# Reading the moving operands of all large products from the last column to the first

## The chip, the cores and the metric

The kernel runs on one core of a Trainium2 chip. A core has a matrix engine (TensorE, PE in the profile, with its weight loads shown apart as PEld), a vector engine (DVE), a scalar engine (ACT), GpSimd (POOL) and SyncE (SP), which issues transfers. They share a scratch memory of 128 partitions (SBUF); TensorE writes its results into an accumulation memory (PSUM) of eight banks of 512 fp32 per partition. The metric is the time of one execution on the device in microseconds (us), the median of several runs.

## The reference

A decoder trunk of two layers for one sequence of 256 tokens with 2048 features, in fp32. Layer 0 mixes tokens with a gated DeltaNet, layer 1 with HGRN2; each mixer and each SwiGLU feed-forward network (FFN, inner width 5632) stands behind an RMS norm and adds to the residual.

```python
def gdn_mixer(h, w_in, conv_w, a_log, dt_bias, head_norm, w_out):
    proj = h @ w_in                      # 2048 -> 12352: q, k, v, z, b, a
    qkv = silu(causal_depthwise_conv(proj[..., :GDN_CONV_DIM], conv_w))
...
    o = gated_delta_rule_chunked(q, k, v, beta, g)
    o = rmsnorm(o, head_norm) * silu(z)
    return o.reshape(B, S, GDN_VAL_DIM) @ w_out

def hgrn2_mixer(h, w_in, lower_bound, head_norm, w_out):
    proj = h @ w_in                      # 2048 -> 8192: q, f, i, gate
...
    return o.reshape(B, S, HGRN_VAL_DIM) @ w_out

def swiglu(h, w_gate, w_up, w_down):
    return (silu(h @ w_gate) * (h @ w_up)) @ w_down
```

Nearly all arithmetic is in these products with weight matrices; the recurrences between them are small products.

## The kernel before

Every weight is streamed once from HBM in tiles of 128 partitions by 1024 columns (`raw`, 512 KB). ACT rounds a tile to TensorE's fast fp32 form (`wh`, type fp32r), and DVE takes the difference, `wl = raw - wh`, in the same form. Activations are split alike into a high and a low half: `xt_h`, `xt_l` for the normed input, `hth`, `htl` for the FFN's inner activations, `ot_h`, `ot_l` for a mixer's output. A product of precise fp32 is then three fast matmuls that accumulate: high by high, high by low, low by high.

In a matmul one operand, the stationary one (128 columns), is loaded into TensorE, and the other, the moving one, is streamed past it column by column; each of its columns gives one column of the output. Each matmul of this kernel brings its own load. There are two forms of large products:

- Rows (`mm_rows`, line 624; `mm_apart`, line 639, calls it in another order for the last group): the stationary operand is 128 tokens of the activations, the moving one 512 columns of the weights. The output has tokens on partitions and features along the row. FFN, the v and z parts of the gated DeltaNet, the v and gate parts of HGRN2, and both output projections are made so. One tile of 1024 columns is two blocks of 512 features with 128 inputs each, so it feeds 2 blocks x 2 halves of the tokens x 3 = 12 matmuls.
- Columns (`mm_cols`, line 652): the stationary operand is 128 features of the weights, the moving one all 256 tokens of the activations. The output has features on partitions and tokens along the row. The q and k parts of the gated DeltaNet and the q and f parts of HGRN2 are made so, with 24 matmuls to a tile.

A third form, `mm_gates`, makes 48 matmuls for the gates. The other products (`aux` tiles) are small and mostly in plain fp32.

The function `layout` (on the host, before the launch) arranges the weights so that each tile is one contiguous block: `tiles` for input projections and FFN, `out_rows` for output projections.

The program is recorded first and then ordered: `Recorder` notes every operation with the region of the tile that it reads or writes (`Virtual.region`, line 107), derives who depends on whom, and plans the order on each engine from estimated costs. The large products keep the order in which they were written; the rest is fitted around them. All operations are issued at one place, line 490, so in the profile nearly every instruction has that line, and groups are told apart by the names of their tiles.

Weight tiles lie in padded buffers (`PAD`, 64 elements), and `make` chooses the offset within the padding: one for tiles of rows products, and one for each half in columns products (`IN_COLS = {"wh": 224, "wl": 512}`, bytes).

These are the three lines of the large products' operands, rows first:

```python
out = ps[tt] if isinstance(ps, tuple) else ps[:, tt, :]
out, s[:, tok], w[:, cols],
ps[:, f // 2, (f % 2) * T : (f % 2 + 1) * T], w[:, at : at + P], s,
```

The second argument is the stationary operand, the third the moving one.

Of the kernel before, what the change touches and what calls it, by code (L numbers as in the profile page):

```python
# [17 lines left out]
P = 128  # L18
T = 256
D = 2048  # L20
# [70 lines left out]
class Virtual:  # L91
# [15 lines left out]
    def region(self, ap):  # L107
        p0, f0 = divmod(ap.offset, self.row)
        p1, f1 = p0 + 1, f0 + 1
        for step, n in ap.ap:  # L110
            if step % self.row:
                f1 += (n - 1) * step
            else:
                p1 += (n - 1) * (step // self.row)
        if f1 > self.row:
            p1, f0, f1 = p1 + (f1 - 1) // self.row, 0, self.row
        if self.pool.space == PSUM:
            return 0, P, 0, self.row
        return p0, p1, f0, f1
# [387 lines left out]
class Trunk:  # L507
# [116 lines left out]
    def mm_rows(self, ps, i, wh, wl, n_chunks, operand, halves=range(2)):  # L624

        for k in range(2):
            xh, xl = operand(2 * i + k)
            cols = slice(k * 512, (k + 1) * 512)
            for tt in halves:
                tok = slice(tt * P, (tt + 1) * P)  # L630
                out = ps[tt] if isinstance(ps, tuple) else ps[:, tt, :]
                for m, (s, w) in enumerate(((xh, wh), (xh, wl), (xl, wh))):
                    self.nc.tensor.matmul(
                        out, s[:, tok], w[:, cols],
                        start=(i == 0 and k == 0 and m == 0),
                        stop=(i == 2 * n_chunks - 1 and k == 1 and m == 2),
                    )
# [14 lines left out]
    def mm_cols(self, ps, i, wh, wl, n_k, n_f, n_chunks):  # L652

        for k in range(n_k):
            kt = i * n_k + k
            xh, xl = self.operand(kt)
            for f in range(n_f):
                at = (k * n_f + f) * P
                for m, (w, s) in enumerate(((wh, xh), (wh, xl), (wl, xh))):
                    self.nc.tensor.matmul(  # L660
                        ps[:, f // 2, (f % 2) * T : (f % 2 + 1) * T], w[:, at : at + P], s,
                        start=(kt == 0 and m == 0 and f % 2 == 0),
                        stop=(i == 2 * n_chunks - 1 and k == n_k - 1 and m == 2),
                        skip_group_check=True,
                    )
# [10 lines left out]
    def operand(self, kt):  # L676
        return self.xt_h[kt // 4][:, kt % 4, :], self.xt_l[kt // 4][:, kt % 4, :]
# [1004 lines left out]
def layout(inputs):  # L1682
    f = lambda n: np.ascontiguousarray(inputs[n])
    out = {}
    x = f("x").reshape(T, D)
    out["x"] = np.ascontiguousarray(x.reshape(2, P, 4, 512).transpose(2, 1, 0, 3))
    cols = lambda v: v.reshape(16, P).T
    ffn_norm = f("ffn_norm")
    norms = [cols(v) for v in (f("gdn_norm")[0], ffn_norm[0], f("hgrn_norm")[0], ffn_norm[1])]
    out["head"] = np.concatenate([np.eye(P, dtype=np.float32)] + norms, 1)  # L1690

    def tiles(w):
        k, g, _ = w.shape
        return np.ascontiguousarray(
            w.reshape(k // 512, 4, P, g, 512).transpose(3, 0, 2, 1, 4)
        ).reshape(g, k // 512, P, 2048)

    for j in range(2):
        gate, up = f("ffn_w_gate")[j], f("ffn_w_up")[j]
        out[f"ffn_gu{j}"] = tiles(  # L1700
            np.stack([gate.reshape(D, N_FF, T), up.reshape(D, N_FF, T)], 2).reshape(D, N_FF, 512)
        )
        lo = 0
        for part, n in enumerate(FF_PARTS):
            rows = f("ffn_w_down")[j][lo * T : (lo + n) * T]
            out[f"ffn_d{j}_{part}"] = tiles(rows.reshape(n * T, 4, 512))
            lo += n
    w = f("gdn_w_in")[0]
    heads = lambda lo: w[:, lo : lo + D].reshape(D, 8, 2, P)
    out["gdn_kq"] = tiles(np.stack([heads(D), heads(0)], 3).reshape(D, 8, 512))  # L1710
    out["gdn_v"] = tiles(w[:, 2 * D : 4 * D].reshape(D, 8, 512))
    out["gdn_z"] = tiles(w[:, 4 * D : 6 * D].reshape(D, 8, 512))
    ba = w[:, 6 * D :].reshape(16, P, 64)
    out["gdn_ba"] = np.ascontiguousarray(ba.transpose(1, 0, 2)).reshape(P, 1024)

    def out_rows(w):
        k = w.shape[0] // 1024
        return np.ascontiguousarray(
            w.reshape(k, 2, 4, P, 4, 512).transpose(0, 4, 1, 3, 2, 5)
        ).reshape(k, 4, 2, P, 2048)  # L1720

    out["gdn_out"] = out_rows(f("gdn_w_out")[0])
    conv = f("gdn_conv")[0]
    out["gdn_conv"] = np.ascontiguousarray(conv[:, : 2 * D].reshape(4, 32, P).transpose(2, 1, 0))
    out["gdn_conv_v"] = np.ascontiguousarray(conv[:, 2 * D :])
    gate = np.stack([f("gdn_a_log")[0], f("gdn_dt_bias")[0]], 1)
    out["gdn_gate"] = np.concatenate([np.zeros_like(gate), gate], 0)
    out["gdn_hn"] = f("gdn_head_norm").reshape(P, 1)
    p, k = np.arange(P)[:, None, None], np.arange(8)[None, :, None]
    out["unit"] = (4 * k + p // 32 == np.arange(32)[None, None, :]).astype(np.float32)  # L1730
    j, i = np.arange(P)[:, None], np.arange(P)[None, :]
    out["hgrn_in"] = tiles(f("hgrn_w_in")[0].reshape(D, 16, 512))
    out["hgrn_out"] = out_rows(f("hgrn_w_out")[0])
    out["hgrn_hn"] = f("hgrn_head_norm").reshape(P, 1)
    out["hgrn_lb"] = np.ascontiguousarray(f("hgrn_lower_bounds").reshape(2, 16, P).transpose(2, 0, 1))
    c = np.arange(CH)[None, :]
    out["masks"] = np.stack(
        [((j >= c // s * 2 * s) & (j < c // s * 2 * s + s)).astype(np.float32) for s in MASKED], 1
    )
    out["final_norm"] = f("final_norm").reshape(1, D)  # L1740
    return out
# [19 lines left out]
```

## Time and profile before

| what | value |
|---|---|
| median of 3 runs | 2774.8 us (2774.77 to 2776.47) |
| span of the profiled execution, first to last instruction | 2773.0 us |
| its mean granted TensorE clock | 0.999 |
| DMA, mean over the span | 209 GB/s, 580.52 MB |

The profile is one execution. Its span leaves out what lies before the first and after the last instruction, 1.8 us against the median. The busy table gives for each engine its busy time, the share of the span and the number of instructions. The chain is the work that ended last, followed back from the end: the engine with the largest share of it sets the time. Groups of instructions show "busy us, mean ns of one | idle time before them, and what ended it". Matmuls are pipelined: one may start while the one before it is still under way, so a group's mean duration is more than what one matmul adds to the time, and the distance from start to start (the pitch) is what counts. Pieces of the chain in order of time are given as start, length, what, and how many instructions.

### The profile page before, as it was taken

How to read it: one execution, taken by the hardware profiler on the slowest of the kernel's cores; microseconds unless marked ns; L12 is line 12 of the kernel's file. 1: busy time of each engine (PE TensorE's matmuls, PEld its weight loads, DVE VectorE, ACT ScalarE, POOL GpSimd, SP SyncE). 2: the span in 40 equal slices, each digit the busy share in tenths (PEclk: the TensorE clock that was granted, in tenths of full speed). 3: DMA queues.
4: the chain of work that ended last, by engine and by line, in shares of the span. 5: the costliest groups of instructions: out<-in, count | busy, mean ns of one | idle time of the engine just before them, and what ended most of it. 6: DMA issues, size and time to landing. Idle time of an engine off the chain costs nothing.

```text
span 2773.0 us, 41091 instructions
## 1 busy us (share of the span) xinstructions
PE 2757.2 (99%) x15662; PEld 2340.8 (84%) x15662; DVE 1901.0 (69%) x2857; ACT 1428.3 (52%) x2010; POOL 251.2 (9%) x370
## 2 busy tenths in 40 slices
PE   9999999999999999999999999999999999999998
PEld 9888888888888888888888989988888888888887
DVE  6787888878766666546665687778656675456764
ACT  6656666565554444344444556556454444344443
POOL 1213222232110000000000100000110000000000
PEclk9999999999999999999999999999999999999999
DMA  7686568786676555666556645545675556665564
GB/s 256 196 280 223 183 214 278 213 276 217 223 255 208 192 195 192 225 222 195 192 194 218 217 164 175 169 166 175 226 265 192 196 192 210 222 208 194 193 201 160
DMA packets 162677, 580.52 MB, mean 209 GB/s; under 512 B 20138, under 2 KB 21306, under 8 KB 162352
## 3 DMA queue, kind: packets, MB, share of 16 engines
q1 hardware_dynamic: 138912, 503.15, 55.4%
q0 software_dynamic: 23280, 73.91, 8.4%
q8 instruction: 122, 2.00, 0.3%
q10 hardware_dynamic: 288, 0.85, 0.1%
q14 instruction: 75, 0.61, 0.1%
HBM read 550.52 MB, written 27.31 MB: 208 GB/s over the span
## 4 chain that ended last, share of the span: by engine, by line
PE 99%; ACT 0%; DVE 0%; issue 0%; POOLq 0%; POOL 0%; ACTq 0%
PE main L490 92%; PE aux L490 6%; ACT dec L490 0%; DVE wl L490 0%; ACT wh L490 0%; ACT xt_h L490 0%; DVE utmp L490 0%; DVE u L490 0%; DVE pre L490 0%; ACT y L490 0%; POOLq L1757 0%; ACT junk L490 0%; DVE xl L490 0%; POOL coll L490 0%; DVE xt_l L490 0%
## 5 line engine op out<-in xcount | busy, mean ns | idle before, releaser
L490 DVE TENSOR_TENSOR wl<-raw,wh 128x1024 fp32r<-128x1024 f32 x945 | 1160.6, 1229 | 759.8 <-ACT wh L490 749.1
L490 ACT ACTIVATE wh<-raw 128x1024 fp32r<-128x1024 f32 x945 | 1000.7, 1060 | 1233.3 <-PE main L490 1137.5
L490 PE MATMUL main<-wh,xt_h 128*128 128x512 f32 x2176 | 849.3, 390 | 0.6 <-ACT wh L490 0.6
L490 PE MATMUL main<-wl,xt_h 128*128 128x512 f32 x2176 | 848.3, 390 | 1.5 <-DVE wl L490 1.5
L490 PE MATMUL main<-wh,xt_l 128*128 128x512 f32 x2176 | 849.5, 390 | 0.0
L490 PEld LDWEIGHTS main<-wl,xt_h 128*128 128x128 f32 x2176 | 408.4, 188 | 85.8 <-DVE wl L490 1.8
L490 PEld LDWEIGHTS main<-wh,xt_h 128*128 128x128 f32 x2176 | 408.5, 188 | 85.1 <-ACT wh L490 1.0
L490 PEld LDWEIGHTS main<-wh,xt_l 128*128 128x128 f32 x2176 | 408.5, 188 | 84.4
L490 PE MATMUL main<-xt_h,wl 128*128 128x256 f32 (+1 forms) x1040 | 292.2, 281 | 1.3 <-DVE wl L490 1.3
L490 PE MATMUL main<-xt_l,wh 128*128 128x256 f32 (+1 forms) x1040 | 291.8, 281 | 0.3 <-DVE xt_l L490 0.3
L490 PE MATMUL main<-xt_h,wh 128*128 128x256 f32 (+1 forms) x1040 | 290.5, 279 | 0.4 <-ACT wh L490 0.4
L490 PE MATMUL main<-wh,htl 128*128 128x512 f32 x664 | 258.6, 389 | 0.0
L490 PE MATMUL main<-wl,hth 128*128 128x512 f32 x664 | 258.3, 389 | 0.0
L490 PE MATMUL main<-wh,hth 128*128 128x512 f32 x664 | 258.3, 389 | 0.0
L490 PEld LDWEIGHTS main<-xt_h,wh 128*128 128x128 f32 (+1 forms) x1040 | 195.6, 188 | 0.9 <-ACT wh L490 0.6
L490 PEld LDWEIGHTS main<-xt_h,wl 128*128 128x128 f32 (+1 forms) x1040 | 193.7, 186 | 1.9 <-DVE wl L490 1.8
L490 PEld LDWEIGHTS main<-xt_l,wh 128*128 128x128 f32 (+1 forms) x1040 | 193.8, 186 | 1.0 <-DVE xt_l L490 0.5
L490 DVE STREAM_TRANSPOSE turned<-h 32x256 f32<-32x256 f32 x352 | 153.5, 436 | 7.2
L490 PE MATMUL main<-wh,ot_l 128*128 128x512 f32 x384 | 151.2, 394 | 0.0
L490 PE MATMUL main<-wh,ot_h 128*128 128x512 f32 x384 | 150.6, 392 | 0.0
L490 PE MATMUL main<-wl,ot_h 128*128 128x512 f32 x384 | 150.5, 392 | 0.0
L490 PEld LDWEIGHTS main<-wl,hth 128*128 128x128 f32 x664 | 124.6, 188 | 25.9
(206 smaller groups left out, 2250.6 us busy)
## 6 DMA issues: line engine op xcount, KB each, us to landing
raw<-in_ffn_gu SPq DMA_DIRECT2D x352, 512.0 KB, 3.7
raw<-in_ffn_d SPq DMA_DIRECT2D x176, 512.0 KB, 4.6
raw<-in_hgrn_in SPq DMA_DIRECT2D x128, 512.0 KB, 3.8
raw<-in_gdn_kq SPq DMA_DIRECT2D x64, 512.0 KB, 5.5
raw<-in_gdn_v SPq DMA_DIRECT2D x64, 512.0 KB, 4.7
raw<-in_gdn_z SPq DMA_DIRECT2D x64, 512.0 KB, 5.0
raw<-in_gdn_out SPq DMA_DIRECT2D x64, 512.0 KB, 5.0
x_home<-x POOLq DMA_DIRECT2D x36, 512.0 KB, 5.7
```

The lines of the kernel that those rows point to most:

```text
L490: getattr(getattr(tc.nc, op.eng), op.method)(*args, **kw)
```

## The change

In both forms of large products the moving operand is read with step minus one, from its last column to its first. In rows products the host lays each block of 512 weight columns out in reverse, so the reversed read gives the columns in natural order. In columns products the activations stay as they are, and the output is addressed in reverse too, so each token lands in its old place. `Virtual.region` learns what a negative step covers.

```diff
@@ Virtual.region
         for step, n in ap.ap:
-            if step % self.row:
+            if step < 0:
+                f0 += (n - 1) * step
+            elif step % self.row:
                 f1 += (n - 1) * step
@@ mm_rows
-                        out, s[:, tok], w[:, cols],
+                        out, s[:, tok], w[:, cols][:, ::-1],
@@ mm_cols
-                        ps[:, f // 2, (f % 2) * T : (f % 2 + 1) * T], w[:, at : at + P], s,
+                        ps[:, f // 2, (f % 2) * T : (f % 2 + 1) * T][:, ::-1], w[:, at : at + P], s[:, ::-1],
@@ layout
-    def tiles(w):
+    def tiles(w, rows=True):
         k, g, _ = w.shape
+        w = w[:, :, ::-1] if rows else w
...
-    out["gdn_kq"] = tiles(np.stack([heads(D), heads(0)], 3).reshape(D, 8, 512))
+    out["gdn_kq"] = tiles(np.stack([heads(D), heads(0)], 3).reshape(D, 8, 512), False)
...
-            w.reshape(k, 2, 4, P, 4, 512).transpose(0, 4, 1, 3, 2, 5)
+            w.reshape(k, 2, 4, P, 4, 512)[..., ::-1].transpose(0, 4, 1, 3, 2, 5)
...
-    out["hgrn_in"] = tiles(f("hgrn_w_in")[0].reshape(D, 16, 512))
+    w = f("hgrn_w_in")[0].reshape(D, 16, 512)
+    out["hgrn_in"] = np.concatenate([tiles(w[:, 0:8], False), tiles(w[:, 8:16])], 0)
```

The 48 matmuls of the gates, the small products and all stationary operands are read as before.

## The prediction

> **What bounds the kernel now.** I read the page's busy table and its chain first, then the waits of TensorE, then the chain in order of time, which gives the pitch (start to start) of the large products.
>
> ```profile
> PE 2757.2 (99%) x15662; PEld 2340.8 (84%) x15662; DVE 1901.0 (69%) x2857; ACT 1428.3 (52%) x2010; POOL 251.2 (9%) x370
> ...
> PEclk9999999999999999999999999999999999999999
> ...
> PE 99%; ACT 0%; DVE 0%; issue 0%; POOLq 0%; POOL 0%; ACTq 0%
> PE main L490 92%; PE aux L490 6%; ACT dec L490 0%; DVE wl L490 0%; ACT wh L490 0%; ACT xt_h L490 0%; DVE utmp L490 0%; DVE u L490 0%; DVE pre L490 0%; ACT y L490 0%; POOLq L1757 0%; ACT junk L490 0%; DVE xl L490 0%; POOL coll L490 0%; DVE xt_l L490 0%
> ```
>
> TensorE is the path: 99% of the span and of the chain, 92% of it in the products that write `main`. The granted clock is full in every slice, so no clock is to be won.
>
> ```profile
> PE main L490 <- DVE wl L490: 2.8, 3, 1.5
> ...
> PE main L490 <- ACT wh L490: 1.0, 2, 0.6
> ```
>
> These are the longest waits of the large products: 3.8 us together. So the time is the number of matmuls times their pitch. The numbers, from the groups by line with shapes kept apart (each group has two sisters with the other operand halves and the same count):
>
> ```profile
> L490 PE MATMUL main<-wh,xt_h 128*128 128x512 f32 x2176 | 849.3, 390 | 0.6 <-ACT wh L490 0.6
> ...
> L490 PE MATMUL main<-xt_h,wh 128*128 128x256 f32 x1024 | 285.8, 279 | 0.4 <-ACT wh L490 0.4
> ...
> L490 PE MATMUL main<-wh,hth 128*128 128x512 f32 x664 | 258.3, 389 | 0.0
> ...
> L490 PE MATMUL main<-wh,ot_h 128*128 128x512 f32 x384 | 150.6, 392 | 0.0
> ...
> L490 PE MATMUL aux<-wh,hth 128*128 128x512 f32 x40 | 15.6, 389 | 0.0
> ```
>
> Rows products of 512 columns: 3 x (2176 + 664 + 384 + 40) = 9,792. Columns products of 256 columns: 3 x 1024 = 3,072. Their durations of 390 and 279 ns are not their cost, since they overlap. The pitch is read from pieces of the chain (start, length, count) in which nothing else stands:
>
> ```profile
> 17.06 17.16 PE main L490 x144
> 34.66 12.00 PE main L490 x102
> 46.92 36.94 PE main L490 x312
> ...
> 638.30 8.86 PE main L490 x38
> ...
> 834.07 636.50 PE main L490 x2808
> ...
> 2048.13 687.72 PE main L490 x3034
> ```
>
> Rows, in both FFNs: 636.50 / 2808 = 687.72 / 3034 = 226.67 ns. Columns, first three pieces: 66.10 / 558 = 118.4 ns. So 9,792 x 0.22667 + 3,072 x 0.1184 = 2219.6 + 363.7 = 2583.3 us of the span of 2773.0 us are what the change touches. The other 189.7 us (small products, start, tail, waits) and the 1.8 us between the span and the median of 2774.8 us stay.
>
> **The change, part by part.** No instruction, transfer or wait is added, removed or moved: on each of the five queues the same instructions stand in the same order with the same waits. What differs is the step of 12,864 moving operands, and, in the 3,072 columns products, of the output as well.
>
> The host's part: weights of the rows products lie reversed in HBM. Each transfer keeps its size and its contiguous lines, the split by ACT and DVE works on whole tiles in either order, and the product comes out in natural column order. Cost nothing, with no cover needed. In the columns products, operand and output are reversed together, so PSUM holds what it held and the evacuations are the same.
>
> The moving read: its cost is 12,864 times the change of the pitch, all of it on the path. No row of this trace reads backwards, so I bound it. Two shapes split the pitch into a share per column and a fixed share: (226.67 - 118.4) / 256 = 0.423 ns per column, and 2 x 118.4 - 226.67 = 10.1 ns that each matmul pays whatever its width. If direction has to do with the fixed share (the read's start, or the weight load that starts with each matmul), the lower bound is that it goes: 12,864 x 10.1 ns = 130 us, 2774.8 - 130 = 2645 us. The same upwards, the fixed share paid twice, is 2905 us. If direction has to do with the share per column (neighbours no longer fetched together), the nearest row is a moving operand that is taken in at a slower rate, the plain fp32 products of the same 512 columns. Their weight loads start with the matmuls, as the other loads do, and tell the pitch:
>
> ```profile
> 84.13 0.19 PEld L490 LDWEIGHTS aux<-kqv 128*128 128x128 f32 x1 [0.24 <-issue]
> 84.56 0.19 PEld L490 LDWEIGHTS aux<-kqv 128*128 128x128 f32 x1 [0.24 <-issue]
> ```
>
> 0.43 us for 512 columns, so about 0.215 us for 256. All products at that rate: 9,792 x 0.43 + 3,072 x 0.215 = 4871 us in place of 2583.3, or 5063 us in all. I take zero for the read: a backward read with step one touches the same words, as many of them, and neighbour after neighbour.
>
> The Trainium skill says the like (SBUF — State Buffer, section "Door 1: The DMA port swizzle"): SBUF is read in lines of 16 bytes and needs at least two hits on a line to hide the access; four fp32 neighbours still share a line in reverse, so by that rule the pitch stays. No run here shows a reversed read yet.
>
> The reversed write into PSUM: with neighbour after neighbour again, I take zero; the upper bound is the columns products alone at the slow rate, 3,072 x (0.215 - 0.1184) = +297 us, or 3072 us in all. Less than zero is not to be had from a write that already follows the pace of the read.
>
> What hides the rest if the products get faster: each weight tile feeds 12 rows products, 2.72 us, and at 216 ns 2.59 us. This is what stands beside them in the first FFN:
>
> ```profile
> core 0: us, PE busy (x) PEld busy (x) DVE busy (x) ACT busy (x) POOL busy (x), PEclk, DMA share, GB/s
> 900.00:1400.00 500.00, 500.00 (x2208) 414.01 (x2207) 308.49 (x359) 214.74 (x227) 5.82 (x8) 1.00 0.62 202
> ```
>
> DVE at 62%, ACT at 43%, and 202 GB/s would go to 65%, 45% and 212 GB/s; none becomes the bound, and a gain in pitch would arrive whole. If the products get slower, all others wait more.
>
> The sum of my forecast: 2583.3 + 189.7 + 1.8 = 2774.8 us, no change.
>
> **The rivals.**
>
> *Faster: the fixed share shrinks.* Each matmul comes with a load of new weights that starts with it:
>
> ```profile
> 1500.07 0.39 PE L490 MATMUL main<-wh,htl 128*128 128x512 f32 x1
> 1500.07 0.19 PEld L490 LDWEIGHTS main<-wh,hth 128*128 128x128 f32 x1
> 1500.30 0.39 PE L490 MATMUL main<-wh,hth 128*128 128x512 f32 x1
> ```
>
> Two reads of one memory start together, 10.1 ns are lost per matmul on both shapes, and the code sets the offsets of its weight tiles by hand. If part of the loss is that the reads get in each other's way, the direction decides where they meet. Half of it gone is 12,864 x 5.05 ns = 65 us: 2710 us; from 0.43 ns per matmul (5.5 us) on it counts. Against it: the pitch in both FFNs is 226.67 ns to the last digit, with other buffers and other work beside, as a loss by collisions would hardly be.
>
> The Trainium skill (TensorE: Matmul & The Clock Gate, section "Step-by-step: what each phase is for") holds against it as well: moving operand and weight load have read ports of their own, and the load steals nothing from the running matmul. By that rule nothing is won. The same page's section "Back-to-back issue gap" gives N / 2.4 + 2.5 ns, 215.8 and 109.2 ns here; were reversal to bring that, the time would be an estimated 2640 us. The trace's 226.67 and 118.4 ns are above both.
>
> *Slower by nanoseconds: the offsets fit a backward read less well.* Same place, opposite sign: where the two reads meet hangs on where their tiles lie, and the reversed operand starts at the far end of its tile. The trace does have pieces with a longer pitch: 8.86 us / 38 = 233.2 ns for rows in the mixer, and 17.16 / 144 = 119.2 ns for columns. If all went there: 9,792 x 6.5 ns + 3,072 x 0.8 ns = 66 us, 2841 us; with the fixed share doubled, 2905 us. It decides from 0.43 ns per matmul too. For it: these pieces show that the pitch isn't wholly fixed. Against it: the longer pieces are few and lie where other products run in between.
>
> *Slower by far: neighbours are fetched together only upwards.* 5063 us, worked out above. For it: 0.423 ns per column is half of the 0.84 ns (0.43 us / 512) of the plain fp32 products, so some doubling is at work in the fast form that could need a step of plus one. Against it: nothing in the trace but symmetry.
>
> *Slower in the columns products alone, through PSUM:* 3072 us. The Trainium skill (PSUM — Partial Sum Buffer, section "Specifications (TRN2)") states lines of 8 bytes, and that any non-contiguous access pattern slows matmuls significantly. Whether a step of minus one counts as that, the page doesn't say, and no run here shows it; in pairs it stays within the lines.
>
> **How the numbers follow.** Chances: no change 0.34, fixed share smaller 0.29, nanoseconds more 0.21, half rate 0.11, PSUM alone 0.05. What a measurement of this kernel can tell from no change is about 0.2%, 5.5 us. So faster 0.29, same 0.34, slower 0.21 + 0.11 + 0.05 = 0.37. No change is the likeliest single case: 2774.8 us, its own range 2769 to 2780. As cases of both signs hold two thirds, the range reaches over both bounds of the fixed share, 2645 to 2905 us; left out are the half rate and PSUM alone, 0.16.
>
> **What would show it.** The two FFN pieces of the chain in the profile after: 2808 and 3034 products at 226.67 ns if I am right; 636.5 us shortened to some 608 if the fixed share goes, lengthened to some 655 if the offsets fit less well, over 1200 if neighbours are not fetched together. In the columns piece 118.4 ns per product; some 215 there with 226.67 in the FFNs would be PSUM alone. The forecast is wrong if either pitch moves by more than half a nanosecond. The shares of DVE and ACT and the GB/s should move only as the span does, and the longest waits of the large products should stay at a few microseconds.

## The result, and the profile after

The changed kernel takes 2839.1 us (median of 4 runs, 2838.18 to 2839.67), beside 2775.56 us for the kernel before in the same comparison: a ratio of 1.0227, 95% interval 1.0213 to 1.0242. It is slower, by 63.5 us.

The page after: busy time of TensorE and its loads, the clock, and the chain by line.

```profile
span 2836.1 us, 41091 instructions
...
PE 2819.8 (99%) x15662; PEld 2343.6 (83%) x15662; DVE 1901.2 (67%) x2857; ACT 1428.5 (50%) x2010; POOL 251.7 (9%) x370
...
PEclk9999999999999999999999999999999999999999
...
PE main L492 92%; PE aux L492 6%; DMA first<-in_x 0%; ACT dec L492 0%; DVE wl L492 0%; ACT wh L492 0%; DVE utmp L492 0%; DVE u L492 0%; SPq L492 0%; DVE pre L492 0%; ACT xt_h L492 0%; ACT y L492 0%; POOLq L1761 0%; ACT junk L492 0%; DVE xl L492 0%
```

The same number of instructions, the same full clock, the same chain. DVE and ACT are busy for the same time as before (1901.2 and 1428.5 us); TensorE's products are busy for 62.6 us more. The longest wait of a large product is still 1.5 us:

```profile
PE main L492 <- DVE wl L492: 2.4, 2, 1.5
```

The chain in order of time (start, length, what, count) says which products became slower:

```profile
46.63 36.95 PE main L492 x312
...
647.43 9.07 PE main L492 x38
...
847.77 655.21 PE main L492 x2808
...
2090.19 707.94 PE main L492 x3034
```

The piece of 38 at 647.43 stands in the first mixer and is taken up further down. Rows products in both FFNs: 655.21 / 2808 = 707.94 / 3034 = 233.3 ns, where it was 226.67. Columns products: 36.95 / 312 = 118.4 ns, as before. 9,792 x 6.67 ns = 65 us; the spans differ by 63.1 us. The remaining 2 us I did not follow.

### The profile page after: what moved, and what is told of

It is laid out like the page before. It is cut to its first block, busy times and chain, and to the rows that moved or that the text cites. A ratio compares the mean times of both kernels' runs of the same rounds, so it can differ in the third digit from the quotient of the medians.

```text
span 2836.1 us, 41091 instructions
## 1 busy us (share of the span) xinstructions
PE 2819.8 (99%) x15662; PEld 2343.6 (83%) x15662; DVE 1901.2 (67%) x2857; ACT 1428.5 (50%) x2010; POOL 251.7 (9%) x370
## 4 chain that ended last, share of the span: by engine, by line
PE 99%; ACT 0%; DVE 0%; issue 0%; DMA 0%; SPq 0%; POOLq 0%; POOL 0%; ACTq 0%
PE main L492 92%; PE aux L492 6%; DMA first<-in_x 0%; ACT dec L492 0%; DVE wl L492 0%; ACT wh L492 0%; DVE utmp L492 0%; DVE u L492 0%; SPq L492 0%; DVE pre L492 0%; ACT xt_h L492 0%; ACT y L492 0%; POOLq L1761 0%; ACT junk L492 0%; DVE xl L492 0%
## 5 line engine op out<-in xcount | busy, mean ns | idle before, releaser
L492 PE MATMUL main<-wh,xt_h 128*128 128x512 f32 x2176 | 867.0, 398 | 0.5 <-ACT wh L492 0.5
L492 PE MATMUL main<-wl,xt_h 128*128 128x512 f32 x2176 | 866.0, 398 | 1.5 <-DVE wl L492 1.5
L492 PE MATMUL main<-wh,xt_l 128*128 128x512 f32 x2176 | 867.2, 399 | 0.0
L492 PEld LDWEIGHTS main<-wh,htl 128*128 128x128 f32 x664 | 124.8, 188 | 30.1
```

Of the source, the lines that this page charges most:

```text
L492: getattr(getattr(tc.nc, op.eng), op.method)(*args, **kw)
```

## Experiments

### Which of the two forms pays

Two kernels with half of the change each. In the first the columns products are read and written forwards again:

```diff
-  ps[:, f // 2, (f % 2) * T : (f % 2 + 1) * T][:, ::-1], w[:, at : at + P], s[:, ::-1],
+  ps[:, f // 2, (f % 2) * T : (f % 2 + 1) * T], w[:, at : at + P], s,
```

> The changed kernel with the columns products (256 wide) read and written forwards again; the 9,792 rows products (512 wide) stay reversed. Theory A (the whole loss sits in the rows products: their pitch went from 226.67 to 233.33 ns, and 9,792 x 6.67 ns = 65 us): about 2839 us, with 233.3 ns in the FFNs and 118 ns in the columns products. Rival B (reversed reads and the reversed write in the columns products cost too, or gain): more than 3 us away from 2839.

In the second, made from the kernel before, only the columns products are reversed:

```diff
-  ps[:, f // 2, (f % 2) * T : (f % 2 + 1) * T], w[:, at : at + P], s,
+  ps[:, f // 2, (f % 2) * T : (f % 2 + 1) * T][:, ::-1], w[:, at : at + P], s[:, ::-1],
```

> The kernel before with only the 3,072 columns products reversed, operand and PSUM output; rows products forwards. Theory A: 2775 us within 3 us, FFN pitch 226.67 ns, columns pitch 118 ns: neither the backward read of 256 columns nor the backward write into PSUM costs anything. Rival B (the write into PSUM in reverse costs, and something else hides it in the changed kernel): above 2780 us and a columns pitch above 119 ns.

Rows alone: 2838.55 us, ratio 1.0228 (1.0211 to 1.0245). Columns alone: 2776.64 us beside 2776.3 us, ratio 1.0001 (0.9991 to 1.001). In the profiles the pitches are 233.3 and 118.4 ns (rows, columns) in the first kernel, 226.7 and 118.4 ns in the second. All of the loss is in the rows products; the backward write into PSUM and, at this kernel's offsets, the backward read of 256 columns cost nothing that can be measured. Theory A held in both.

### Series of matmuls, one property at a time

A kernel that holds nothing but series of matmuls of the fast fp32 form, on real weights, as sets of three with a high and a low half of each operand:

```python
for i in range(count):
    low_w, low_x = i % 3 == 1, i % 3 == 2
    tc.nc.tensor.matmul(
        ap(ps, 512, 0, n, ostep),
        ap(xf, ROW_X, sat + 4096 * low_x, P, sstep),   # stationary
        ap(wf, ROW_W, mat + 8192 * low_w, n, mstep),   # moving
        start=i == 0, stop=i == count - 1)
```

A series' name tells what it is: f or r (forwards, reversed), columns, m and the moving offset, s and the stationary offset (both modulo 1024), k and the stationary step where it isn't one, and at the end o where the output is reversed. A stationary operand in reverse was not tried. This kernel and the three like it below were run once each, at a granted clock of 0.998 to 0.999.

> Computes nothing of the reference: 78 series of 60 matmuls of the same fast fp32 form, each series with its own width, direction of the moving read, offsets of both operands (bytes modulo 1024) and step of the stationary operand; TensorE does nothing else. Theory C (the offsets fit a backward read less well, as the rival in the prediction had it): at offset 32 the 512-wide series take 226.7 ns forwards and 233.3 ns backwards, and some other offset of the moving or stationary operand brings the backward read to 227 ns or less. Theory D (the weight load is itself read from its last column to its first, so a backward moving read runs along with it and meets it longer): the loss hangs on how fast the load walks; with a stationary step of 0 (no walk) both directions are alike, and with steps of 2 and 4 the difference between directions changes size. Theory E (a backward read has a fixed price of 8 cycles of 0.833 ns whatever stands beside it): 233.3 ns at every offset and every stationary step, and 6.7 ns more at 320, 384 and 448 columns too.

Rows of the timeline, start, length, series, count; the pitch is the distance to the next start over 60:

```profile
31.77 13.80 PE L134 MATMUL f512m32s32e<-wf,xf 128*128 128x512 f32 x60
45.41 14.17 PE L134 MATMUL r512m32s32e<-wf,xf 128*128 128x512 f32 x60
59.42 14.07 PE L134 MATMUL f512m32s32k0e<-wf,xf 128*128 128x512 f32 x60
73.33 14.17 PE L134 MATMUL r512m32s32k0e<-wf,xf 128*128 128x512 f32 x60
...
214.24 13.78 PE L134 MATMUL f512m32s32o<-wf,xf 128*128 128x512 f32 x60
227.86 14.17 PE L134 MATMUL r512m32s32o<-wf,xf 128*128 128x512 f32 x60
...
501.58 14.15 PE L134 MATMUL f512m64s32e<-wf,xf 128*128 128x512 f32 x60
515.57 14.16 PE L134 MATMUL r512m64s32e<-wf,xf 128*128 128x512 f32 x60
529.57 13.91 PE L134 MATMUL f512m96s32e<-wf,xf 128*128 128x512 f32 x60
...
808.70 14.15 PE L134 MATMUL f512m32s64e<-wf,xf 128*128 128x512 f32 x60
822.69 14.17 PE L134 MATMUL r512m32s64e<-wf,xf 128*128 128x512 f32 x60
```

Forwards at the kernel's offsets: (45.41 - 31.77) / 60 = 227.3 ns with the first few, 226.7 ns once it runs steadily. Backwards: 14.01 / 60 = 233.5 ns. So the small series show what the kernel shows. With the moving operand at 64, forwards too takes 13.99 / 60 = 233.2 ns, and the same where the stationary operand alone is moved to 64. Backwards stays where it was. With a stationary step of 0, where the load reads one place over and over, forwards is at 13.91 / 60 = 231.8 ns; with step 2 at 233.3 and with step 4 at 234.9, once steady, while backwards it is 233.3 ns with all four steps. A reversed output alone (`f512m32s32o`) costs nothing.

Theory C is half right: the good offset is lost, but none of the other offsets tried brought the backward read to 227 ns. Theory D has for it that the walk of the load matters to a forward read, and against it that it doesn't to a backward one, and that the two directions still differ by 1.5 ns with step 0. Theory E fails at 320 columns, with 146.7 ns in both directions once steady; at 384 and 448 columns a backward read takes 4 ns more, not 6.7; and at moving offsets that are no multiple of 16 bytes (4, 8 and 12) it takes 235.6 to 240.1 ns.

An offset and the one 256 bytes on have the same pitch (moving 32 and 288: 226.7 ns both, 192 and 448: 234.3 ns both), so from here on offsets are counted modulo 256.

### Every pair of offsets

The same series with 24 matmuls, for all 256 pairs of offsets in steps of 16 bytes modulo 256, in both directions.

> Computes nothing of the reference: 512 series of 24 matmuls of 512 columns, every pair of a moving and a stationary offset in steps of 16 bytes modulo 256, first all forwards, then all backwards. Theory C2 (the pitch of a forward read hangs on the distance between the two offsets, a backward read has one price): forwards from 226.7 ns on a few pairs, 32 and 32 among them, to some 234 or more on most; backwards 233.3 ns on nearly every pair and 226.7 ns on none. Rival C (backward reads have good offsets too, the change only missed them): some pairs at 227 ns or less backwards.

Part of the timeline, moving offset 32, stationary 32 to 80, forwards, and then 32 and 48 backwards (pitch: distance of starts over 24):

```profile
220.32 5.60 PE L569 MATMUL f512m32s32e<-wf,xf 128*128 128x512 f32 x24
225.76 5.61 PE L569 MATMUL f512m32s48e<-wf,xf 128*128 128x512 f32 x24
231.21 5.75 PE L569 MATMUL f512m32s64e<-wf,xf 128*128 128x512 f32 x24
236.80 5.76 PE L569 MATMUL f512m32s80e<-wf,xf 128*128 128x512 f32 x24
...
1642.90 5.77 PE L569 MATMUL r512m32s32e<-wf,xf 128*128 128x512 f32 x24
1648.50 5.76 PE L569 MATMUL r512m32s48e<-wf,xf 128*128 128x512 f32 x24
```

From the starts of all series, leaving out the first eight matmuls of each: forwards from 226.7 to 236.8 ns, half of the pairs above 232.7, and 54 of 256 below 228; the pitch repeats when both offsets move by 32 together, within 0.7 ns but for 7 pairs. Backwards from 233.1 to 236.7 ns, 225 of 256 within half a nanosecond of 233.3, and none below 233. The offsets that the kernel's rows products have, 32 and 32, are one of the 54. Theory C2 held in what it says of the good pairs, and rival C fell for all pairs tried. Its sizes were off: only 10 forward pairs take 234 ns or more, not most. And the distance alone doesn't decide: at distance 0 the pitch is 226.7 ns where both offsets are multiples of 32, and mostly 233.3 where they lie 16 bytes further on.

### The same in the whole kernel

The weight tiles of the rows products (and of the 48 gate products) at 64 in place of 32, in the kernel before and in the changed one (every second buffer at 64 + 256, which is 64 modulo 256; before, it was 32 + 512):

```diff
-  want = IN_COLS[v.tag] if v.cols else 32 + n % 2 * 512
+  want = IN_COLS[v.tag] if v.cols else 64 + n % 2 * 256
```

> The kernel before, forwards, with the weight tiles of the rows products moved from offset 32 to offset 64 (modulo 256); the activations stay at 32. Theory C2 (the change lost a good offset and nothing more): in the series a forward read at this distance took 233.2 ns, so 9,792 x 6.6 ns = 65 us more than before, about 2841 us, as slow as the changed kernel. Rival E (backward reads have a price of their own, on top of any offset): the kernel before doesn't care, 2776 us.

> The changed kernel with the weight tiles of the rows products moved from offset 32 to offset 64 (modulo 256) as well. Theory C2: a backward read takes 233.3 ns at either distance, so 2839 us, within 3 us of the changed kernel and of the forward kernel at this offset. Rival E (a price on top of any offset): a further 65 us, about 2904 us. Rival C (another offset fits a backward read): clearly below 2839 us.

The forward kernel at 64: 2837.37 us, ratio to the kernel before 1.0227 (1.021 to 1.0244). The changed kernel at 64: 2838.42 us, ratio 1.0229 (1.0214 to 1.0245). One piece of the chain for each, forwards first:

```profile
846.83 655.20 PE main L490 x2808
```

```profile
847.90 655.21 PE main L492 x2808
```

233.3 ns in both. Moving the tiles from 32 to 64 costs the forward kernel what the reversal cost, and costs the reversed kernel nothing. This settles where the loss of the change comes from: it gave up a good pair of offsets, and no pair tried gives a backward read of 512 columns that pitch.

### Is it the load's length

Shorter weight loads, to see whether what a matmul pays beyond its columns is the time in which the two reads overlap.

> Computes nothing of the reference: series of 60 matmuls with 128, 96, 64 and 32 stationary columns, 512 and 256 moving columns, four moving offsets, both directions; then 128 series of 30 matmuls of 256 columns in which the offsets of the stationary operand's high and low halves are swept. Theory F (what a matmul pays beyond its columns, and the price of the direction, come from the reads of the next weight load meeting the moving read): with a load of 32 columns both directions and all offsets fall together at 512 columns, within 2 ns, and well below 226 ns. Rival G (a price of changing weights, whatever the load reads): 226.7 ns forwards at offset 32 and 233.3 ns backwards with every number of stationary columns.

Series with 32 stationary columns (c32) at moving offsets 32 and 64:

```profile
536.39 14.05 PE L249 MATMUL f512m32s32c32e<-wf,xf 128*32 128x512 f32 x60
550.28 14.16 PE L249 MATMUL r512m32s32c32e<-wf,xf 128*32 128x512 f32 x60
564.29 14.14 PE L249 MATMUL f512m64s32c32e<-wf,xf 128*32 128x512 f32 x60
578.26 14.17 PE L249 MATMUL r512m64s32c32e<-wf,xf 128*32 128x512 f32 x60
```

Theory F fell at 512 columns: with a quarter of the load, the pitch is 231.5 and 232.8 ns forwards and 233.5 backwards, not well below 226. Rival G holds for the backward read, but for 2 of its 16 series (236.6 and 236.7 ns), and not for the forward one, whose good offsets go elsewhere: with 96 columns 64 is the good one (226.7 ns) and 32 is not (230.0), with 64 columns it is 192. At 256 moving columns the quarter of the load does shorten the forward pitch, from 116.6 to 120.0 ns on the four moving offsets to 113.3 ns on three of them and 117.3 on the fourth; backwards it is 117.8 ns on all four. So what the load reads does shift a forward read's pitch, but the price is no simple sum of collisions. The second part, 256 columns, had one pair of stationary offsets well below the others: high at 96, low at 224, with 113.3 ns where the kernel's pair, 224 and 0, has 117.8. The same pair forwards and backwards (the pitch is the distance to the next start over 30):

```profile
813.51 3.57 PE L249 MATMUL f256m32s96l224e<-wf,xf 128*128 128x256 f32 x30
816.91 3.70 PE L249 MATMUL f256m32s128l0e<-wf,xf 128*128 128x256 f32 x30
...
1040.42 3.70 PE L249 MATMUL r256m32s96l224e<-wf,xf 128*128 128x256 f32 x30
1043.95 3.69 PE L249 MATMUL r256m32s128l0e<-wf,xf 128*128 128x256 f32 x30
```

Forwards it is 113.3 ns, backwards 117.7, and none of the 64 backward pairs is below 117.6. So a backward read has no good pair among those tried at 256 columns either. The columns products lost nothing because their pair, at 117.8 ns in both directions, was not a good one to begin with.

### Other widths, other types, and a faster kernel

> Computes nothing of the reference: 256 series of 24 matmuls of 256 columns forwards, every pair of offsets of the stationary operand's high and low halves in steps of 16 bytes, the moving operand at 32; then widths of 288 to 512 in both directions at moving offsets 32 and 64; then bf16 and plain fp32 operands in both directions. Theory E2 (a backward read costs up to 8 cycles of 0.833 ns more than the best forward pair, whatever the load does, and only where the moving read and not the load sets the pitch): from 384 columns on the backward series take 4 to 7 ns more than the forward ones at 32, nothing more at 288 and 320, and 0 to 1 ns more than the forward ones at 64. Rival H (the price comes with 4-byte elements read at full rate): bf16 and plain fp32 show no difference between the directions beyond 1 ns; under E2 alone bf16 would show it as well.

Rows of the timeline at 416 columns, and in bf16 (bf) and plain fp32 (pl, two records to a matmul):

```profile
905.70 11.36 PE L351 MATMUL f416m32s32e<-wf,xf 128*128 128x416 f32 x60
916.90 11.63 PE L351 MATMUL r416m32s32e<-wf,xf 128*128 128x416 f32 x60
928.36 11.76 PE L351 MATMUL f416m64s32e<-wf,xf 128*128 128x416 f32 x60
939.96 11.50 PE L351 MATMUL r416m64s32e<-wf,xf 128*128 128x416 f32 x60
...
1108.48 13.12 PE L374 MATMUL bff512m32e<-wb,xb 128*128 128x512 bf16 x60
1121.66 13.11 PE L374 MATMUL bfr512m32e<-wb,xb 128*128 128x512 bf16 x60
...
1188.23 15.72 PE L374 MATMUL plf512m32e<-wr,xr 128*128 128x512 f32 x36
1204.01 15.72 PE L374 MATMUL plr512m32e<-wr,xr 128*128 128x512 f32 x36
```

In bf16 and in plain fp32 both directions have the same rows, 13.12 and 13.11 us, and 15.72 us twice. Within the series the pitch is 215.8 ns in bf16 and 429.2 ns for a record of plain fp32, in both directions and at both offsets: of the offsets tried, direction and offset matter only to the fast fp32 form, as rival H had it. Theory E2 failed in part: at 416 columns and offset 64 the backward read is the faster one, 188.9 against 193.4 ns once steady, and at 384 columns and 64 the slower, 180.0 against 176.7. At offset 32, where the kernel's tiles lie, it is the slower one by 2 to 7 ns at every width from 352 columns on. A backward read has no fixed price of its own; what it lacks, at 512 and at 256 columns, is a good pair.

The pair 96 and 224 in the kernel before, forwards:

```diff
-IN_COLS = {"wh": 224, "wl": 512}
+IN_COLS = {"wh": 96, "wl": 480}
```

> The kernel before, forwards, with the weight tiles of the columns products at offsets 96 (high) and 480, which is 224 modulo 256 (low), in place of 224 and 512. In the series of 256 columns this pair took 113.3 ns against 117.8 ns at the kernel's pair. If the distance between the two reads sets the columns products' pitch as it does in the rows products (theory C2): 3,072 x 4.5 ns = 14 us less, about 2762 us. Rival I (the series are too tidy; in the kernel the load of the next weights sets the pitch of the columns products anyway): 2776 us within 3 us.

2764.54 us beside 2776.44 us, ratio 0.9955 (0.9941 to 0.9968): faster than both kernels of this study. Its piece of the columns products and one of the rows products:

```profile
45.49 35.62 PE main L490 x312
...
831.20 636.50 PE main L490 x2808
```

35.62 / 312 = 114.2 ns in place of 118.4, and the rows untouched; 3,072 x 4.2 ns = 13 us, of which 12 arrive. So in the columns products too the offsets set the pitch, and rival I fell. A series is not the last word at 256 columns, though: of the 64 pairs that stand in both kernels of series, 10 differ between them by more than 0.7 ns. High and low both at 96 took 117.8 ns in one and 113.4 in the other, and the pair 96 and 224 needed eight matmuls to settle in the second. So the pitch there depends in part on what ran before.

## Why the prediction was wrong

The forecast was no change; the time came out where the rival "slower by nanoseconds" was priced.

- *What bounds the kernel, and the counts.* Right. The pitch of 9,792 products carried all of the loss.
- *The fixed share of 10.1 ns.* A misreading, on which the lower and the upper bound and the rival "faster" rest. It compares 226.67 ns, a good pair of its width, with 118.4 ns, which is no good pair of its own; with the best pair found at each width 2 x 113.3 - 226.7 leaves nothing.
- *No instruction, transfer or wait moves; nothing beside the products costs.* Right: DVE and ACT are busy for the same time to within 0.2 us.
- *"I take zero for the read: a backward read with step one touches the same words, as many of them, and neighbour after neighbour."* This step failed. It asks what is read, and not what is read beside it. The pitch of the rows products is 226.7 ns on some pairs of offsets of the moving and the stationary operand and longer on the rest; forwards the kernel had one of the good pairs, and backwards at 512 columns no pair tried is one. In place of zero the term was 9,792 x 6.67 ns = 65 us.
- *"Against it: the pitch in both FFNs is 226.67 ns to the last digit, with other buffers and other work beside, as a loss by collisions would hardly be."* This reading led there. The pitch is constant because all rows products have their operands at the same offsets modulo 256, whatever the buffer. Moving the tiles by 32 bytes moved that constant to 233.3 ns. A constant pitch speaks for constant conditions, not against a dependence on them.
- *Slower by nanoseconds, 2841 us.* Right in place (the offsets of the rows tiles) and close in size, but the size was luck. It was taken from a piece with 233.2 ns in the mixer, and in the profile after that piece reads 9.07 / 38 = 238.7 ns, so its 6.5 ns were on top. The timeline before shows where they come from, at the start of the piece, right behind small products:

```profile
638.23 0.50 PE L490 MATMUL main<-wl,xt_h 128*128 128x512 f32 x1
638.57 0.40 PE L490 MATMUL main<-wh,xt_l 128*128 128x512 f32 x1
```

The first step takes 0.34 us, and some products later the pitch is 226.7 ns as everywhere. So 233.2 ns was the mean of one slow start and a usual pitch. And the offsets don't fit "less well": at 512 columns, in steps of 16 bytes, 225 of 256 pairs take a backward read the same 233.3 ns and none takes less than 233.
- *Slower by far.* Fell: the FFN piece takes 655.21 us, not over 1200. Its price was also read from one record of a plain fp32 product, and such a product has two of 429.2 ns each.
- *The columns products, and the write into PSUM.* Right at zero, and for the read that hung on the kernel's pair: in the series, 4.4 ns separate the directions at 96 and 224. The rule of the Trainium skill (PSUM — Partial Sum Buffer, section "Specifications (TRN2)"), that any non-contiguous pattern slows matmuls, doesn't bite at a step of minus one: the kernel with the columns products alone reversed has a ratio of 1.0001.
- *The rules weighed.* The Trainium skill (SBUF — State Buffer, section "Door 1: The DMA port swizzle") has neighbours in one line at full rate, and by it I expected no change. The series agree in bf16 and in plain fp32, at the offsets tried, and at 256 columns at the kernel's pair; at 512 columns of the fast form the trace disagrees, 233.3 against 226.7 ns. By the Trainium skill (TensorE: Matmul & The Clock Gate, section "Step-by-step: what each phase is for") the load steals nothing from the running matmul, which I counted against any effect of where the reads meet. The series disagree: the stationary offset alone takes the pitch from 226.7 to 233.3 ns. What passes between the two reads, no run shows.

Left open: what the steps of 6.67 ns are made of, and why no backward read tried, at 512 or at 256 columns, gets the shorter one. A load that runs along with the backward read would explain it, but the series with step 0 and with short loads show no sign of it.

## What to carry to other kernels

Where TensorE is the bound and the pitch is a few per cent above that of another type, vary the offsets of moving and stationary operand against each other before anything else: a series of 24 matmuls per pair and one profile show all pairs, and the kernel itself confirms the best ones, since a series can depend on the one before it. A pitch that is constant everywhere may be constant because every tile was aligned alike. And a part on which an edit costs nothing may only have had nothing to lose. An edit of the direction, the padding or the buffers of a tuned operand is also an edit of its offset, and has to be priced as one.

## What was not expected of the hardware

The pitch of the fast fp32 form hangs on where the stationary operand lies beside the moving one: 226.7 to 236.8 ns for the same 512 columns forwards, 113.3 to 124.7 ns for 256. Backwards the lower end is missing: 233.1 and 117.6 ns are the least. bf16 and plain fp32 show nothing of this at two moving offsets. At 256 columns a stationary step of 4 doubles the pitch (233.3 ns); at 512 columns it adds 8 ns at most.
